# Weight sums moved to VectorE, residual rows scaled around an MLP in place of 1/rms inside it, and one more running sum through GpSimd

## The chip, the cores and the metric

The kernel runs on one core of a Trainium2 chip. The metric is the device time of one execution in microseconds (us), as the median of several runs. The engines are named as in the profile: PE is TensorE, DVE is VectorE, ACT is ScalarE, POOL is GpSimd, and SP issues most DMAs.

## The reference

One step of a two-layer streaming encoder over 1024 prompt frames and 32 sample frames, 1056 tokens of width 1024, all in float32. Each layer adds a token mixer and an MLP to the residual stream, both behind an RMS norm:

```python
def rmsnorm(x, g):
    y = x * lax.rsqrt(jnp.mean(x * x, axis=-1, keepdims=True) + EPS)
    return y * g
...
for i in range(DEPTH):                       # DEPTH = 2
    a = rmsnorm(h, norm_mix[i])
    h = h + mixer(a)                         # HGRN2 recurrence in layer 0, short convolution in layer 1
    m = rmsnorm(h, norm_mlp[i])
    h = h + jnp.square(jax.nn.relu(m @ w_up[i])) @ w_down[i]     # 1024 -> 4096 -> 1024
return rmsnorm(h, norm_final), ...
```

What matters here is the MLP. Its norm is a factor of one token: with v the mean square plus EPS, m is h times the norm's weights over sqrt(v). Relu and square carry a positive factor of a token through, so the square of the relu carries a factor 1/v.

## The kernel before

The tokens lie along the free axis, the features on the 128 partitions. The residual is eight tiles `hT[m]` of 128x1056. A float32 operand of a matmul is split in a high and a low part in `float32r` (`part`: ScalarE makes the high part as a cast, VectorE the low part as a difference), and a product is three matmuls (low times high, high times low, high times high; `mm3`, `mm_half`).

**The MLP.** The 4096 features are taken in 16 chunks of 256. A chunk has an `up` stage, which makes two tiles `u` of 128x1056, and two `down` stages, one for each half of the output features. Both use a Strassen scheme on 2x2 blocks, so they need sums of weight blocks (`wsums`) and sums of data blocks (`xsums`, called by `sums`). The order of the stages, written out at the end of `mlp`, is up(0), sums(0), up(1), down(0, 0), down(0, 1), sums(1), up(2), and so on. The loads and splits of a stage's weights are issued two stages ahead. Layer 0 ends with the last chunk in a plain product (`plain`), which hands each finished row of hT to the next norm and to the convolution; layer 1 ends with the last two chunks in a plain product over three groups of tokens (`groups`), behind which the final norm runs.

**`wsums`** loads 128x1024 weights (one of two `raw` tiles), splits the first half and the third quarter, then makes four sums of quarters (128x256) in place on GpSimd, and splits what they give. `whi` and `wlo` have seven buffers each.

**`up`** evicts eight results into four half tiles of `u` (`READ`): the first of a half is copied by ScalarE, later ones are added by VectorE, and when a half is complete VectorE takes relu and multiplies by 1/rms (`nrm.r`), and ScalarE squares. The chunk 0 of a layer is evicted raw and finished later, since its matmuls run before 1/rms is there: `nrm.scale`, called in the midst of chunk 0's matmuls, sums the squares over partitions by a matmul with ones and takes three Newton steps (`rsqrt`) on VectorE, each pass over 128x1056.

**`down`** computes seven products (`STEPS`) for two row halves p each, alternating p. PSUM has four tiles of two banks (`pb`). Products 0, 2, 4 and 6 of one p accumulate in tile a, 1 and 3 in tile b, and 5 is tile c. After each product its tile is read and added to, or subtracted from, a half row of hT (`TO` names row and half: product 0 and 5 go to block (0, 0), 2 and 3 to (0, 1), 1 and 4 to (1, 1), 6 to (1, 0)). VectorE does this straight from PSUM, except for products 0 and 6: ScalarE copies these to `st` (four buffers), and GpSimd adds them.

Each engine runs its own queue in order. The order in the queues is made by a planner from the order of the program, the dependencies and its own costs; only the start of the program (SP) is ordered by hand.

Of the kernel before, what the change touches and what calls it, by code (L numbers as in the profile page):

```python
# [8 lines left out]
F32 = mybir.dt.float32  # L9
# [4 lines left out]
AF = mybir.ActivationFunctionType  # L14
# [21 lines left out]
def trunk_kernel(  # L36
# [94 lines left out]
    def gsl(g):  # L131
        c0, n = GROUPS[g]
        return slice(c0, c0 + n), n
# [550 lines left out]
    class Norm:  # L684
# [13 lines left out]
                nc.gpsimd.tensor_tensor(self.acc, self.acc, sq, op=ALU.add)  # L698
            self.n += 1

        def scale(self):
            v = self.new("nv")
            _, pss = trio()
            for g in range(3):
                sl, n = gsl(g)
                ps = pss[g]
                nc.tensor.matmul(ps[:, :n], ones, self.acc[:, sl], start=True, stop=True)
                nc.vector.tensor_scalar(v[:, sl], ps[:, :n], 1.0 / D, EPS, op0=ALU.mult, op1=ALU.add)
            r = mp.tile([P, NTOK], F32, tag="nr", name="nr")
            rsqrt(v, r, self.acc)  # L710
            self.r = r
# [39 lines left out]
    def wsums(src):  # L751

        raw = wraw(src)
        t = lambda i: raw[:, i * 256 : (i + 1) * 256]
        hl = [wpart(raw[:, :512]), wpart(t(2))]
        for d, o in ((2, 3), (3, 0), (0, 2), (1, 0)):
            nc.gpsimd.tensor_tensor(t(d), t(d), t(o), op=ALU.add)  # L757
# [87 lines left out]
    def mlp(layer, nrm, on_final, last, X):  # L845
# [3 lines left out]
        def up(c):  # L849
            def run(w):  # L850
                u = [ut("u") for j in range(2)]
                left = {b: list(READ.values()).count(b) for b in READ.values()}
                made = set()

                def read(what, ps):
                    i, h = b = READ[what]
                    sl = slice(h * HALF, (h + 1) * HALF)
                    d = u[i][:, sl]
                    op0 = ALU.min if i else ALU.max
                    left[b] -= 1  # L860
                    src = d
                    if b in made:
                        nc.vector.tensor_tensor(q2(d), q2(d), ps, op=ALU.add)
                    elif left[b] or c == 0:
                        nc.scalar.copy(q2(d), ps)
                    else:
                        src = ps
                    made.add(b)
                    if not left[b]:
                        r = lambda: nrm.r[:, sl]  # L870

                        def end():
                            if src is d:
                                nc.vector.scalar_tensor_tensor(d, d, 0.0, r(), op0=op0, op1=ALU.mult)
                            else:
                                nc.vector.scalar_tensor_tensor(q2(d), src, 0.0, q2(r()), op0=op0, op1=ALU.mult)
                            if c:
                                nc.scalar.activation(d, d, AF.Square)
                            else:
                                nc.vector.tensor_tensor(d, d, d, op=ALU.mult)  # L880

                        later.append(end) if c == 0 else end()

                later = []
# [4 lines left out]
                for f in later:  # L889
                    f()  # L890
                U[c] = u

            return lambda: wpair(Wu[c]), run
# [9 lines left out]
        def down(c, b):  # L903
            def run(w):
                x = Z[c]
                ps = [{}, {}]
                for i, (bank, f, g, start) in enumerate(STEPS):
                    for p in range(2):
                        if start:
                            ps[p][bank] = pt()  # L910
                        t = ps[p][bank]
                        mm_half(t, w(f, p), x[g], start, True)
                        v = t[:, :, :QT]
                        r, h, op = TO[i]
                        d = hT[4 * b + 2 * p + r][:, h * HALF : (h + 1) * HALF]
                        if i in (0, 6):
                            st = mp.tile([P, HALF], F32, tag="st", name="st", bufs=4)
                            nc.scalar.copy(q2(st), v)  # L918
                            nc.gpsimd.tensor_tensor(d, d, st, op=op)  # L919
                        else:  # L920
                            nc.vector.tensor_tensor(q2(d), q2(d), v, op=op)  # L921

            return lambda: wsums(Wd[c, b]), run

        def wblocks(src):
# [2 lines left out]
            hl = [wpart(raw[:, i * 512 : (i + 1) * 512]) for i in range(2)]  # L928
            return lambda i, j, p: wcut(hl[BLK[(i, j)] // 2], BLK[(i, j)] % 2 * 2 + p)

        def plain(b):


            def run(w):
                for m in range(4 * b, 4 * b + 4):
                    a, pss = trio()
                    mm_groups(pss, [w(m % 2, j, m % 4 // 2) for j in range(2)], G)
                    nc.vector.tensor_tensor(two(hT[m]), two(hT[m]), a[:, :, :384], op=ALU.add)
                    nc.vector.tensor_tensor(hT[m][:, 768:], hT[m][:, 768:], pss[2][:, :288], op=ALU.add)
                    on_final(m)  # L940

            return lambda: wblocks(Wd[NFC - 1, b]), run
# [8 lines left out]
        def gsplit(u, new):  # L951
            h, l = [new(t, F32R) for t in ("gh", "gl")]
            part(h, l, u)
            G.append((h, l))


        def groups():


            n = NFC - 2  # L960

            def prep():
                wts = []
                for i in range(4):
                    raw = wraw(Wd[n + i % 2, i // 2])
                    h, l = [t[:, :1024] for t in xpair()]
                    part(h, l, raw)
                    wts.append((h, l))
                return wts

            def run(wts):
                for g in range(3):
                    c0, nt = FGROUPS[g]
                    sl = slice(c0, c0 + nt)
                    pss = {}
                    order = [(m, k) for m in range(KT) for k in range(4)]
                    if g == 0:
                        order = [(m, k) for m in range(4) for k in range(3)] + [(m, 3) for m in range(4)] + order[16:]
                    for m, k in order:
                        if k == 0:  # L980
                            pss[m] = newps()[:, :nt]
                        w = wcut(wts[m // 4 * 2 + k // 2], 2 * BLK[(m % 2, k % 2)] + m % 4 // 2)
                        gh, gl = G[k]
                        mm3(pss[m], *w, gh[:, sl], gl[:, sl], k == 0, k == 3)
                        if k == 3:
                            nc.vector.tensor_tensor(hT[m][:, sl], hT[m][:, sl], pss[m], op=ALU.add)
                            on_final(g, m)

            return prep, run
# [22 lines left out]
        ready = [work[0][0](), work[1][0]()]  # L1012
# [216 lines left out]
```

## Time and profile before

| what | value |
|---|---|
| median of 3 runs | 2498.72 us (2497.92 to 2499.29) |
| time of the profiled execution | 2497.78 us |
| its span | 2495.6 us |
| mean granted clock | 0.988 |
| busy PE, DVE, ACT, POOL | 2395.5, 1747.7, 917.1, 848.7 us |

The MLPs lie at about 625 to 1375 us and 1740 to 2495 us of the span. A row of a group of instructions gives line, engine, operation, written and read tiles with shapes and a count; behind the bar stand the busy time in us, the mean of one in ns, and the idle time of the engine just before these instructions with what ended it. A row of a timeline gives start and duration in us, and in brackets the idle time before it with its releaser. A row of waits gives who waited for whom, total us, times, and the longest.

### The profile page before, as it was taken

How to read it: one execution, taken by the hardware profiler on the slowest of the kernel's cores; microseconds unless marked ns; L12 is line 12 of the kernel's file. 1: busy time of each engine (PE TensorE's matmuls, PEld its weight loads, DVE VectorE, ACT ScalarE, POOL GpSimd, SP SyncE). 2: the span in 40 equal slices, each digit the busy share in tenths (PEclk: the TensorE clock that was granted, in tenths of full speed). 3: DMA queues.
4: the chain of work that ended last, by engine and by line, in shares of the span. 5: the costliest groups of instructions: out<-in, count | busy, mean ns of one | idle time of the engine just before them, and what ended most of it. 6: DMA issues, size and time to landing. Idle time of an engine off the chain costs nothing.

```text
span 2495.6 us, 42858 instructions
## 1 busy us (share of the span) xinstructions
PE 2395.5 (96%) x17700; PEld 2345.9 (94%) x17700; DVE 1747.7 (70%) x2842; ACT 917.1 (37%) x1671; POOL 848.7 (34%) x920
## 2 busy tenths in 40 slices
PE   8999999989899999999999999999999999999998
PEld 8999999989899999999999999999999999999997
DVE  8775757554878777787788633354887787787875
ACT  5121212133344444444445111143344444444444
POOL 3110101012255454545555000002255554555433
PEclk9999999999999999999999999999999999999999
DMA  4111010031011111111111111111111111111111
GB/s 148 38 32 44 29 46 23 28 114 38 32 47 47 52 52 43 43 52 43 50 45 51 51 51 44 43 51 35 35 51 43 43 52 44 54 49 43 51 52 70
DMA packets 35779, 122.22 MB, mean 49 GB/s; under 512 B 4336, under 2 KB 7552, under 8 KB 35584
## 3 DMA queue, kind: packets, MB, share of 16 engines
q1 hardware_dynamic: 33632, 113.58, 14.5%
q0 software_dynamic: 1952, 5.92, 0.6%
q8 instruction: 138, 2.26, 0.4%
q14 instruction: 57, 0.47, 0.1%
HBM read 114.09 MB, written 5.39 MB: 48 GB/s over the span
## 4 chain that ended last, share of the span: by engine, by line
PE 74%; POOL 8%; issue 8%; DVE 8%; ACT 2%; DMA 0%; DVEq 0%; SPq 0%; POOLq 0%; ACTq 0%
PE pb L807 34%; PE pb L115 6%; PE pb L117 6%; PE pb L116 6%; POOL hT L919 6%; PE pj L115 4%; PE pj L116 3%; PE pj L117 3%; DVE wlo L601 2%; POOL raw L757 2%; PE v L501 1%; PE v L503 1%; PE v L502 1%; PE aps L394 1%; ACT whi L600 1%
## 5 line engine op out<-in xcount | busy, mean ns | idle before, releaser
L600 ACT CAST whi<-raw 128x512 fp32r<-128x512 f32 (+1 forms) x476 | 275.3, 580 | 867.0 <-PE pb L807 450.5
L757 POOL TENSOR_TENSOR raw<-raw 128x256 f32<-128x256 f32 x360 | 371.4, 1032 | 365.5 <-DVE wlo L601 237.7
L601 DVE TENSOR_TENSOR wlo<-raw,whi 128x512 fp32r<-128x512 f32 (+1 forms) x476 | 362.4, 763 | 186.7 <-ACT whi L600 180.9
L919 POOL TENSOR_TENSOR hT<-hT,st 128x528 f32<-128x528 f32 x232 | 329.4, 1431 | 335.9 <-ACT st L918 335.9
L921 DVE TENSOR_TENSOR hT<-hT,pb 128x528 f32<-128x528 f32 x580 | 387.4, 696 | 19.5 <-PE pb L807 14.5
L807 PE MATMUL pb<-B,whi 128*128 128x264 f32 x2160 | 356.0, 287 | 0.0
L115 PE MATMUL pb<-xh,wlo 128*128 128x384 f32 (+1 forms) x960 | 312.3, 325 | 5.8 <-DVE wlo L601 5.8
L117 PE MATMUL pb<-xh,whi 128*128 128x384 f32 (+1 forms) x960 | 310.9, 324 | 0.0
L116 PE MATMUL pb<-xl,whi 128*128 128x384 f32 (+1 forms) x960 | 309.9, 323 | 0.8 <-DVE xl L604 0.8
L807 PEld LDWEIGHTS pb<-B,whi 128*128 128x128 f32 x2160 | 303.5, 191 | 0.0
L807 PE MATMUL pb<-B,wlo 128*128 128x264 f32 x1080 | 228.0, 293 | 11.5 <-DVE hT L921 7.6
L807 PE MATMUL pb<-T,whi 128*128 128x264 f32 x1440 | 238.2, 288 | 0.0
L807 PE MATMUL pb<-Q,whi 128*128 128x264 f32 x1440 | 235.1, 285 | 0.0
L807 PE MATMUL pb<-xh,wlo 128*128 128x264 f32 x1024 | 208.4, 285 | 0.0
L807 PE MATMUL pb<-xl,whi 128*128 128x264 f32 x1024 | 208.2, 285 | 0.0
L807 PE MATMUL pb<-xh,whi 128*128 128x264 f32 x1024 | 207.7, 284 | 0.0
L807 PEld LDWEIGHTS pb<-T,whi 128*128 128x128 f32 x1440 | 203.9, 193 | 0.0
L807 PEld LDWEIGHTS pb<-Q,whi 128*128 128x128 f32 x1440 | 200.5, 190 | 0.0
L807 PE MATMUL pb<-Q,wlo 128*128 128x264 f32 x720 | 150.9, 291 | 42.3 <-ACT st L918 42.3
L807 PEld LDWEIGHTS pb<-B,wlo 128*128 128x128 f32 x1080 | 169.0, 190 | 23.6 <-DVE hT L921 18.3
L115 PEld LDWEIGHTS pb<-xh,wlo 128*128 128x128 f32 x960 | 181.0, 189 | 6.2 <-issue 5.9
L115 PE MATMUL pj<-xh,wlo 128*128 128x384 f32 (+1 forms) x536 | 176.6, 330 | 6.7 <-ACT xh L192 6.7
(265 smaller groups left out, 4857.3 us busy)
## 6 DMA issues: line engine op xcount, KB each, us to landing
raw<-in_wg_up_dram SPq DMA_DIRECT2D x64, 512.0 KB, 3.5
raw<-in_wg_down_dram SPq DMA_DIRECT2D x64, 512.0 KB, 3.6
raw<-in_wg_in_hgrn_dram SPq DMA_DIRECT2D x31, 512.0 KB, 4.1
raw<-in_wg_cu_conv_dram SPq DMA_DIRECT2D x16, 512.0 KB, 3.5
xk<-in_x_t_dram SPq DMA_DIRECT2D x8, 528.0 KB, 8.2
hT<-in_x_t_dram POOLq DMA_DIRECT2D x8, 528.0 KB, 8.1
raw<-in_wg_out_hgrn_dram SPq DMA_DIRECT2D x8, 512.0 KB, 4.6
raw<-in_wg_b_conv_dram SPq DMA_DIRECT2D x8, 512.0 KB, 3.4
```

Of the source, the lines that this page charges most:

```text
L115: nc.tensor.matmul(ps, wlo, ah, start=start, stop=False)
L116: nc.tensor.matmul(ps, whi, al, start=False, stop=False)
L117: nc.tensor.matmul(ps, whi, ah, start=False, stop=stop)
L394: nc.tensor.matmul(o, H.K[:, sl], H.F[:, sl], start=True, stop=True)
L501: nc.tensor.matmul(o, al, hi[:, kk], start=(k == 0), stop=False)
L502: nc.tensor.matmul(o, ah, lo[:, kk], start=False, stop=False)
L600: nc.scalar.copy(h, src)
L601: nc.vector.tensor_tensor(l, src, h.bitcast(F32), op=ALU.subtract)
L757: nc.gpsimd.tensor_tensor(t(d), t(d), t(o), op=ALU.add)
L807: nc.tensor.matmul(ps[:, q, :QT], w, half(v, q), start=start and n == 0, stop=stop and n == 2, skip_group_check=True)
L919: nc.gpsimd.tensor_tensor(d, d, st, op=op)
L921: nc.vector.tensor_tensor(q2(d), q2(d), v, op=op)
```

## The change

With v the mean square of a token, the kernel now keeps v itself (`nrm.mean`) and no 1/rms in an MLP. The up stages take relu of the raw result (the negated half through a scale of -1) and square it, both on ScalarE, in chunk 0 as in the others. The result of the down products is then too large by v for each token, so all eight rows of hT are multiplied by v on GpSimd, behind chunk 0's up stage and ahead of the first running sum, and at the end multiplied by 1/v: `inverse` makes the reciprocal in place on VectorE, and `plain` and `groups` multiply behind each last eviction. `Norm.scale` stays for the convolution's norm. Besides, the four sums of `wsums` are on VectorE instead of GpSimd, and product 2 of a `down` stage goes through ScalarE and GpSimd like 0 and 6.

```diff
+        def mean(self):
+            v = mp.tile([P, NTOK], F32, tag="nr", name="nr")
+            self.means(v)
+            self.v = v
+
+        def means(self, v):
             _, pss = trio()
             for g in range(3):
                 ...
                 nc.tensor.matmul(ps[:, :n], ones, self.acc[:, sl], start=True, stop=True)
                 nc.vector.tensor_scalar(v[:, sl], ps[:, :n], 1.0 / D, EPS, op0=ALU.mult, op1=ALU.add)
 ...
         for d, o in ((2, 3), (3, 0), (0, 2), (1, 0)):
-            nc.gpsimd.tensor_tensor(t(d), t(d), t(o), op=ALU.add)
+            nc.vector.tensor_tensor(t(d), t(d), t(o), op=ALU.add)
 ...
-                    elif left[b] or c == 0:
+                    elif left[b]:
 ...
                     if not left[b]:
-                        ...  nc.vector.scalar_tensor_tensor(d, d, 0.0, r(), op0=op0, op1=ALU.mult)
-                        ...  nc.scalar.activation(d, d, AF.Square)      # chunk 0: on VectorE, later
+                        nc.scalar.activation(q2(d), src, AF.Relu, scale=-1.0 if i else 1.0)
+                        nc.scalar.activation(d, d, AF.Square)
 ...
-                    mm_pair(w, X, read, LATE, {2: nrm.scale})
+                    mm_pair(w, X, read, LATE, {2: nrm.mean})
+                    for m in range(KT):
+                        nc.gpsimd.tensor_tensor(hT[m], hT[m], nrm.v, op=ALU.mult)
 ...
-                        if i in (0, 6):
+                        if i in (0, 2, 6):
                             st = mp.tile([P, HALF], F32, tag="st", name="st", bufs=4)
                             nc.scalar.copy(q2(st), v)
                             nc.gpsimd.tensor_tensor(d, d, st, op=op)
 ...
+        def inverse():
+            for g in range(3):
+                sl, _ = gsl(g)
+                nc.vector.reciprocal(nrm.v[:, sl], nrm.v[:, sl])
 ...                                                     # plain
+                    nc.vector.tensor_tensor(hT[m], hT[m], nrm.v, op=ALU.mult)
                     on_final(m)
 ...                                                     # groups
+                            nc.vector.tensor_tensor(hT[m][:, sl], hT[m][:, sl], nrm.v[:, sl], op=ALU.mult)
                             on_final(g, m)
 ...                                                     # stages: last layer, first layer
+            stages.append(inverse)
             stages.append(up(n + 1))
 ...
-            stages += [down(n - 1, 1), plain(0), plain(1)]
+            stages += [down(n - 1, 1), inverse, plain(0), plain(1)]
```

More of the change, by code (lines that the diff above doesn't have):

```diff
@@ L699, in add @@
             self.n += 1
-        def scale(self):
-            v = self.new("nv")
+        def mean(self):
[3 more added lines that the diff above has]
+        def means(self, v):
             _, pss = trio()
@@ L708, in scale @@
                 nc.vector.tensor_scalar(v[:, sl], ps[:, :n], 1.0 / D, EPS, op0=ALU.mult, op1=ALU.add)
+        def scale(self):
+            v = self.new("nv")
+            self.means(v)
             r = mp.tile([P, NTOK], F32, tag="nr", name="nr")
@@ L856, in read @@
                     i, h = b = READ[what]
-                    sl = slice(h * HALF, (h + 1) * HALF)
-                    d = u[i][:, sl]
-                    op0 = ALU.min if i else ALU.max
+                    d = u[i][:, h * HALF : (h + 1) * HALF]
                     left[b] -= 1
-                    src = d
+                    src = q2(d)
                     if b in made:
-                        nc.vector.tensor_tensor(q2(d), q2(d), ps, op=ALU.add)
-                    elif left[b] or c == 0:
-                        nc.scalar.copy(q2(d), ps)
+                        nc.vector.tensor_tensor(src, src, ps, op=ALU.add)
+                    elif left[b]:
+                        nc.scalar.copy(src, ps)
                     else:
```

14 lines of the change are left out of this document (removed).

## The prediction

> **What bounds the kernel now.** The page's first part comes first: it says which engine the time belongs to.
>
> ```profile
> span 2495.6 us, 42858 instructions
> PE 2395.5 (96%) x17700; PEld 2345.9 (94%) x17700; DVE 1747.7 (70%) x2842; ACT 917.1 (37%) x1671; POOL 848.7 (34%) x920
> ```
>
> TensorE (PE) is busy for 2395.5 of 2495.6 us, so about 100 us of idle time is all that any schedule can win, unless it takes matmuls away, which this change does not. Where the 100 us lie, the windows over single chunks and the list of waits say (in a window row the columns are length, then PE, weight load, VectorE, ScalarE and GpSimd busy time, granted clock, DMA share and rate; in a wait row total, times, longest).
>
> ```profile
> 818.96:863.92 44.96, 43.17 (x351) 42.53 (x350) 35.42 (x54) 20.49 (x37) 23.57 (x20) 1.00 0.15 48
> 1843.00:1888.00 45.00, 43.20 (x351) 42.56 (x351) 35.55 (x54) 20.58 (x38) 23.61 (x21) 1.00 0.15 48
> ...
> PE pb L807 <- ACT st L918: 42.3, 28, 1.5
> PEld pb L807 <- DVE hT L921: 18.9, 51, 0.6
> ACT whi L600 <- POOL raw L757: 83.1, 34, 2.6
> ```
>
> A chunk of an MLP takes 45.0 us, of which PE idles 1.8. There are 29 chunks with a down stage (232 GpSimd running sums, 8 per chunk, in the group rows below), so 52 us of the 100 are this one stall. The timeline of one chunk shows what it is made of:
>
> ```profile
> 869.08 0.69 DVE L601 TENSOR_TENSOR wlo<-raw,whi 128x512 fp32r<-128x512 f32 x1
> ...
> 875.94 0.74 POOL L757 TENSOR_TENSOR raw<-raw 128x256 f32<-128x256 f32 x1
> 876.62 1.31 POOL L919 TENSOR_TENSOR hT<-hT,st 128x528 f32<-128x528 f32 x1
> 876.71 0.62 ACT L600 CAST whi<-raw 128x512 fp32r<-128x512 f32 x1 [2.58 <-POOL raw L757]
> 877.24 0.59 ACT L918 COPY st<-pb 128x528 f32<-128x528 f32 x1
> 877.36 1.12 DVE L601 TENSOR_TENSOR wlo<-raw,whi 128x512 fp32r<-128x512 f32 x1 [4.20 <-ACT whi L600]
> 877.88 0.51 PE L807 MATMUL pb<-Q,wlo 128*128 128x264 f32 x2 [1.51 <-ACT st L918]
> ```
>
> The cast of summed weights stands ahead of an eviction copy in ScalarE's queue and waits 2.58 us for GpSimd's weight sums; the copy behind it is late, so PE waits 1.51 us for its PSUM bank, and VectorE, 4.20 us idle, then evicts late (the short waits on L921).
>
> **The change part by part.** The durations (busy us, mean ns):
>
> ```profile
> L921 DVE TENSOR_TENSOR hT<-hT,pb 128x528 f32<-128x528 f32 x580 | 387.4, 696 | 19.5 <-PE pb L807 14.5
> L757 POOL TENSOR_TENSOR raw<-raw 128x256 f32<-128x256 f32 x360 | 371.4, 1032 | 365.5 <-DVE wlo L601 237.7 <-issue 111.0
> L919 POOL TENSOR_TENSOR hT<-hT,st 128x528 f32<-128x528 f32 x232 | 329.4, 1431 | 335.9 <-ACT st L918 335.9
> L918 ACT COPY st<-pb 128x528 f32<-128x528 f32 x232 | 136.0, 598 | 20.6 <-PE pb L807 15.1
> L601 DVE TENSOR_TENSOR wlo<-raw,whi 128x256 fp32r<-128x256 f32 x90 | 37.4, 416 | 5.2 <-ACT whi L600 5.2
> L874 DVE SCALAR_TENSOR_TENSOR u<-u,nr 128x528 f32<-128x528 f32 x98 | 69.3, 711 | 0.2
> L878 ACT ACTIVATE u<-u 128x528 f32<-128x528 f32 x120 | 77.6, 647 | 48.4 <-DVE u L874 46.4 <-DVE u L876 1.9
> L698 POOL TENSOR_TENSOR acc<-acc,sq 128x1056 f32<-128x1056 f32 x21 | 54.5, 2597 | 178.2 <-ACT sq L697 178.1
> L285 DVE RECIPROCAL R<-F 128x384 f32<-128x384 f32 x16 | 40.1, 2530 | 0.2
> ```
>
> Budget of a steady chunk. VectorE: 12 weight sums come (three weight sets of four; priced like the 128x256 split, 0.416) = +5.0; four evictions go to ScalarE = -2.8; four relu-times-1/rms go = -2.8: together -0.6 of 35.4. GpSimd: 12 x 1.032 go, 4 x 1.431 come = -6.7 of 23.6. ScalarE: 4 x 0.598 + 4 relu at the price of a square, 0.647 = +5.0 on 20.5, of 45. No engine becomes the bound by its total, so the sum is decided by waits.
>
> *The wait that goes.* The sums follow the 128x256 split on VectorE without another engine in between, some 0.34 us apart, so the cast is ready about 2 us earlier and the 1.8 us per chunk disappear. What is late next is the point.
>
> *The wait that comes.* In a down stage PE computes seven products for each of two row halves, alternating. Product 2 and product 3 both add into the same block (0, 1) of hT. Before, VectorE did both. Now product 2 goes ScalarE copy, GpSimd add, and VectorE's add of product 3 must wait for that add. Product 5 needs the PSUM tile that this add of product 3 releases (four tiles: two hold products 0, 2, 4, 6 to the end, two are product 1 and 3's). So each half has a new chain GpSimd to VectorE to PE, and the next evictions are queued behind the blocked one on VectorE. Its clock comes from these rows:
>
> ```profile
> 885.27 22.92 PE pb L807 x186
> ...
> 863.65 0.31 PEld L807 LDWEIGHTS pb<-Q,wlo 128*128 128x128 f32 x2
> 863.92 2.81 POOL L919 TENSOR_TENSOR hT<-hT,st 128x528 f32<-128x528 f32 x2 [0.20 <-ACT st L918]
> 864.69 4.36 DVE L921 TENSOR_TENSOR hT<-hT,pb 128x528 f32<-128x528 f32 x6 [0.43 <-PE pb L807]
> 874.65 1.34 POOL L919 TENSOR_TENSOR hT<-hT,st 128x528 f32<-128x528 f32 x1
> 885.56 3.20 POOL L919 TENSOR_TENSOR hT<-hT,st 128x528 f32<-128x528 f32 x2 [4.38 <-ACT st L918]
> ```
>
> PE needs 6 x 22.92/186 = 0.74 us for a product of one half, and a product is ready 1.04 us after its load begins (863.65 to 864.69). GpSimd adds follow each other every 1.29 us when undisturbed (874.65 to 875.94).
>
> Second down of a chunk, with 0 where its first product is ready: the preceding down's two last products are ready at -1.48 and -0.74 and go to GpSimd too. Six adds, the first at -0.86 (copy 0.6), end at -0.86 + 6 x 1.29 = 6.9; VectorE's add of product 3, second half, ends at 7.6; PE wants the tile for product 5, second half, at 11 x 0.74 - 1.04 = 7.1. Stall 0.5 at least.
>
> Now the port. At 877.36 the split took 1.12 us where the 128x512 form took 0.69 at 869.08: it ended 0.55 us after GpSimd's add that ran until 877.93. The reverse is seen here:
>
> ```profile
> 892.33 0.41 DVE L601 TENSOR_TENSOR wlo<-raw,whi 128x256 fp32r<-128x256 f32 x1
> 892.67 0.69 DVE L776 TENSOR_TENSOR u<-u 128x528 f32<-128x528 f32 x1
> 892.88 2.95 POOL L757 TENSOR_TENSOR raw<-raw 128x256 f32<-128x256 f32 x1 [4.11 <-issue]
> ```
>
> A 0.74 us add took 2.95 us while VectorE streamed SBUF sums. The four new weight sums (start to start 0.34, as 892.33 to 892.67) and a split (about 0.6) fall into that second down and hold GpSimd off by up to 4 x 0.34 + 0.6 = 2.0 us: stall 0.5 to 2.5. I take 2.0, since the 128x256 split that they follow ends just before that stage's first product. The Trainium skill, "SBUF — State Buffer", section "Who interferes with whom", says that a VectorE instruction with two SBUF inputs and a GpSimd instruction that reads SBUF exclude each other, the later one blocking fully; 1.12 against 0.69 agrees. By that rule the stall is at the 2.5 end, without it at 0.5, and the total moves between +35 and -23 us for the 29 chunks.
>
> First down of a chunk: only four adds, from about 1.2 after its own zero (its copies now stand behind a relu in ScalarE): end 6.4, VectorE 7.1, wanted 7.1: stall 0 to 0.5, taken 0.2. Its last evictions follow later and the next down's first tile needs them: 0 to 1.0, taken 0.3.
>
> Sum per chunk: 2.5 (0.5 to 4.0) comes, 1.8 goes: +0.7 (-1.3 to +2.2), times 29 = **+20 us** (-38 to +64).
>
> *MLP heads.* The mean replaces the rsqrt: nine VectorE passes of 128x1056 (1.25 us each, the row of L147 below) go, 11 us, and the first chunk's four squarings. There PE waits:
>
> ```profile
> PE pb L707 <- POOL acc L698: 5.2, 1, 5.2
> PE pb L807 <- DVE u L863: 2.4, 2, 1.9
> ```
>
> The 5.2 us stay: the sum of squares still ends on GpSimd, and the matmul for the mean keeps its place. The 2.4 go. Against them come eight GpSimd products of hT and the mean, priced as L698, 21 us, before the first down, on the port that the splits and sums use: taken as 0 net, -5 to +10 for both heads.
>
> *End of layer 0.* The last down is the plain product, eight rows of hT:
>
> ```profile
> 1325.00:1371.00 46.00, 44.07 (x292) 43.05 (x291) 41.49 (x46) 26.32 (x33) 25.93 (x13) 1.00 0.17 56
> L604 DVE SCALAR_TENSOR_TENSOR xl<-hT,vec,xh 128x1056 fp32r<-128x1056 f32 x8 | 18.4, 2303 | 1.0 <-ACT xh L603 1.0
> L147 DVE TENSOR_TENSOR acc<-nv,nr 128x1056 f32<-128x1056 f32 x9 | 11.3, 1253 | 0.2
> ```
>
> VectorE is busy 41.5 of 46 here, and its split of a row takes 2.3 us, being held by GpSimd's sums of squares. Eight products of a row, priced at the 1.25 of the same shape, stand between eviction and split, and the convolution cannot start its last row before: +10 us, 5 where PE's own queue hides half, 17 if the three reciprocals (2.53 each, 7 with the narrow one) fall here. I expect those earlier, in VectorE's gaps: +1 for both layers.
>
> *End of layer 1.* 24 products, one behind each eviction:
>
> ```profile
> 2440.00:2460.00 20.00, 20.00 (x121) 19.59 (x120) 11.09 (x32) 10.78 (x20) 2.23 (x3) 1.00 0.02 6
> 2481.93 0.41 DVE L986 TENSOR_TENSOR hT<-hT,pb 128x256 f32<-128x256 f32 x1
> ```
>
> VectorE has 9 of 20 us free, so PE hides most; the last one, 0.41 like the eviction, is in the tail. +2 (0.4 to 5).
>
> Sum: 20 + 0 + 10 + 1 + 2 = +33 us on the profiled execution's 2497.8 (2.2 of it outside the span) = 2531; the median of the runs shown is 0.9 higher, so 2532.
>
> **The rivals.** *Faster: the queue stall goes and GpSimd delivers in time.* If the weight sums land after the six adds, the chunk's stall is 0.5 + 0.2 + 0.1 = 0.8, -1.0 x 29 = -29; heads -5, end of layer 0 +5: 2470. For it speaks that GpSimd's total falls by 6.7 us a chunk; against it that six adds in a row leave no reserve even undisturbed (7.6 against 7.1). It decides from a stall below 1.4 us per chunk, where 29 x 0.4 pay for the 12 us at the ends.
>
> *VectorE's queue becomes the bound in the down stages.* If a split or sum is queued between the two adds of product 3, the late evictions pile up: the stall reaches 4.0, +64, with 15 at the end of layer 0: 2579. For it speaks that its evictions run at PE's own pace now (six in 4.36 us, 0.73 each); against it the 2 us gap that the moved product 2 leaves.
>
> *Nothing to measure.* 1.4 us per chunk cancels the ends: 2499. It needs a coincidence.
>
> **How the numbers follow.** A measurement can tell about 0.2%, 5 us. Chances: forecast and neighbourhood (2512 to 2555) 0.40, VectorE's queue 0.17, no change 0.10, faster 0.33. Likeliest 2532, alone 2512 to 2555. For 8 in 10 the range must take in most of both rivals: 2468 to 2570.
>
> **What would show it.** In the changed profile the wait of the cast on L757's GpSimd sums is gone; a wait of VectorE's L921 on GpSimd's L919 appears, some 58 to 116 times, and PE waits on L921 grow from 18.9 us to 50 or more; a chunk takes 45.7 us (45.0 now); the stretch from the last down of layer 0 to the convolution grows by 10 us. I am wrong if chunks fall below 44.5 us: then either the adds are not held, or the order on VectorE puts the sums elsewhere. If the end of layer 0 does not grow, VectorE had more room there than 41.5 of 46 says.

## The result, and the profile after

| | before | after |
|---|---|---|
| median | 2498.6 us (4 runs) | 2653.16 us (4 runs, 2649.05 to 2655.59) |
| ratio, 95% interval | | 1.0617 (1.0599 to 1.0635) |
| profiled execution: time, span | 2497.78, 2495.6 us | 2653.62, 2651.8 us |
| mean granted clock | 0.988 | 0.959 |

The change costs 154 us. The forecast was 2532 us, at most 2570: the direction was right, the size was not. The first part of the page after:

```profile
span 2651.8 us, 43088 instructions
PE 2467.1 (93%) x17700; PEld 2407.9 (91%) x17700; DVE 1871.5 (71%) x2968; ACT 1059.9 (40%) x1921; POOL 705.1 (27%) x692
```

TensorE has the same 17700 matmuls, yet it is busy for 72 us longer (2467.1 against 2395.5): part of its work ran slower. The rest of the 156 us is idle time. GpSimd is less busy than before (705 against 849 us), VectorE more by 124 us. That last number is the surprise, since the forecast's budget had VectorE 0.6 us a chunk lower. The groups say where it comes from (busy us, mean ns, then idle):

```profile
L915 POOL TENSOR_TENSOR hT<-hT,st 128x528 f32<-128x528 f32 x348 | 504.6, 1475 | 921.6 <-ACT st L914 918.5
L917 DVE TENSOR_TENSOR hT<-hT,pb 128x528 f32<-128x528 f32 x464 | 318.3, 699 | 163.9 <-PE pb L816 82.7
L766 DVE TENSOR_TENSOR raw<-raw 128x256 f32<-128x256 f32 x360 | 250.0, 695 | 7.1
```

A weight sum takes 0.695 us on average, where 0.416 was assumed; the evictions (L917) kept their 0.70.

The matmuls come in the same order in all kernels here, so two traces can be laid side by side at the n-th matmul. The table gives the time of a stretch of matmuls, less that of the kernel before, in us. The experiments are in it too. A chunk is 348 matmuls, so each column of chunks holds about 13 of them. Left out are the stretch between head and chunks of layer 0 (matmul 4560 to 5040), from -4.7 to +0.9, the one between the layers (10080 to 12240), from -0.8 to +4.4, and what lies ahead of the first head, at most 2.0 either way.

| kernel | head, layer 0 (4320-4560) | 13 chunks (5040-9600) | end, layer 0 (9600-10080) | head, layer 1 (12240-12720) | 13 chunks (12720-17280) | last part (17280-17699) |
|---|---|---|---|---|---|---|
| before, us | 30.1 | 595.5 | 80.6 | 66.2 | 592.5 | 67.6 |
| **after** | **+11.5** | **+53.6** | **+11.6** | **+11.2** | **+55.9** | **+10.7** |
| e1_sums_on_pool | +12.8 | +40.5 | +11.6 | +11.8 | +40.1 | +11.8 |
| e2_products06 | +11.6 | +18.8 | +8.4 | +8.2 | +22.0 | +10.2 |
| e3_sums_only | -0.6 | +19.7 | 0.0 | -0.2 | +19.7 | 0.0 |
| e4_norm_only | +12.8 | +3.4 | +8.9 | +9.5 | +3.6 | +11.8 |
| e5_no_sums | +10.8 | +0.7 | +11.8 | +7.2 | +1.2 | +8.1 |
| e6_late_inverse | +8.8 | +3.4 | +16.9 | +4.1 | +3.2 | +11.8 |
| e7_half_sums | +10.6 | +19.2 | +12.2 | +7.3 | +20.0 | +10.5 |
| e8_free_start | +11.6 | -5.5 | +10.8 | +8.4 | -4.4 | +10.7 |
| e9_pool_order | -0.7 | -35.0 | 0.0 | -2.4 | -34.2 | 0.0 |
| e10_head_halves | +10.9 | +53.9 | +11.7 | +6.6 | +54.4 | +12.4 |
| e11_no_products | -0.7 | +53.5 | +11.7 | -0.2 | +54.8 | +9.5 |
| e12_no_division | +3.3 | +54.8 | +3.5 | +2.8 | +54.5 | +0.1 |

So 110 of the 156 us lie in the steady chunks, and the heads and ends cost 45 us.

**A chunk.** Windows of ten chunks of layer 0, from the 5448th matmul on (length, then PE, weight load, VectorE, ScalarE, GpSimd busy; granted clock; DMA share and rate), before and after:

```profile
788.90:1242.39 453.49, 435.64 (x3481) 429.87 (x3481) 356.96 (x531) 204.64 (x360) 235.21 (x201) 0.99 0.16 47
```

```profile
808.67:1303.50 494.83, 455.49 (x3481) 447.00 (x3481) 394.23 (x570) 250.02 (x440) 173.43 (x120) 0.95 0.14 43
```

A chunk grew from 45.35 to 49.48 us: TensorE idles 3.93 us instead of 1.79 in it, and is busy 1.99 us longer, at a lower clock. The waits (total, times, longest) of after name who makes it idle:

```profile
PEld pb L816 <- DVE hT L917: 116.7, 91, 3.3
PE pb L816 <- DVE hT L917: 94.3, 61, 3.1
DVE hT L917 <- POOL hT L915: 80.4, 60, 2.6
PE pb L816 <- ACT st L914: 14.7, 28, 0.5
...
ACT whi L600 <- DVE raw L766: 49.4, 32, 1.6
```

TensorE waits for VectorE's evictions: 28 pauses of about 3.1 us, one in a second down stage of a chunk, make up 86.5 of the 94.3 us. The timeline of VectorE and GpSimd around one such pause:

```profile
798.87 0.70 DVE L917 TENSOR_TENSOR hT<-hT,pb 128x528 f32<-128x528 f32 x1
799.49 5.33 DVE L766 TENSOR_TENSOR raw<-raw 128x256 f32<-128x256 f32 x4
804.73 1.78 DVE L601 TENSOR_TENSOR wlo<-raw,whi 128x512 fp32r<-128x512 f32 x1
806.44 1.30 DVE L917 TENSOR_TENSOR hT<-hT,pb 128x528 f32<-128x528 f32 x2
...
798.59 9.09 POOL L915 TENSOR_TENSOR hT<-hT,st 128x528 f32<-128x528 f32 x6 [3.76 <-ACT st L914]
...
803.13 1.40 POOL L915 TENSOR_TENSOR hT<-hT,st 128x528 f32<-128x528 f32 x1
803.40 1.42 DVE L766 TENSOR_TENSOR raw<-raw 128x256 f32<-128x256 f32 x1
...
836.30 1.81 DVE L766 TENSOR_TENSOR raw<-raw 128x256 f32<-128x256 f32 x4
...
807.18 0.81 PE L816 MATMUL pb<-B,wlo 128*128 128x264 f32 x2 [3.09 <-DVE hT L917]
```

The four weight sums of the next up stage take 5.33 us here and 1.81 us where GpSimd is idle (836.30). Look at the single pair: GpSimd's add runs from 803.13 to 804.53, VectorE's sum is issued at 803.40 and ends at 804.82, just behind it. Each sum, and the split behind them, waits out one GpSimd add (the first sum, which takes 0.95 us, only the rest of one). The evictions of product 1 stand behind these five instructions in VectorE's queue and start at 806.44, and TensorE has been idle for 3.09 us by then. An eviction, which reads PSUM, runs at its full speed while GpSimd's last add goes on (806.44, two in 1.30 us).

The same pause in windows of 2 us shows what follows it:

```profile
802.00:804.00 2.00, 1.50 (x11) 1.17 (x10) 1.97 (x2) 1.56 (x3) 1.95 (x2) 1.00 0.00 0
804.00:806.00 2.00, 0.09 (x1) 0.00 (x0) 2.00 (x2) 0.60 (x1) 2.00 (x3) 1.00 0.00 0
806.00:808.00 2.00, 0.82 (x3) 0.82 (x4) 1.74 (x3) 0.00 (x0) 1.68 (x1) 0.55 0.00 0
808.00:810.00 2.00, 2.00 (x11) 2.00 (x11) 0.70 (x1) 0.00 (x0) 0.00 (x0) 0.50 0.00 0
810.00:812.00 2.00, 2.00 (x11) 2.00 (x11) 1.70 (x3) 0.62 (x1) 0.00 (x0) 0.50 0.00 0
812.00:814.00 2.00, 2.00 (x14) 2.00 (x14) 1.38 (x3) 1.13 (x2) 0.00 (x0) 0.75 0.41 156
814.00:816.00 2.00, 2.00 (x19) 2.00 (x18) 1.70 (x4) 1.56 (x4) 0.00 (x0) 1.00 0.26 107
```

From the end of the pause on the granted clock is 0.50 for nearly 7 us, and TensorE starts 11 matmuls in 2 us instead of 19. In the ten chunks of the windows the clock stood at one half for 51.1 us, and for 10.0 us before. Half of the 41 us more is 20.5 us, close to the 19.9 us that TensorE was busy longer.

### The profile page after: what moved, and what is told of

The parts are those of the page before. It is cut to its first block, busy times and chain, and to the rows that moved or that the text cites. A ratio compares the mean times of both kernels' runs of the same rounds, so it can differ in the third digit from the quotient of the medians.

```text
span 2651.8 us, 43088 instructions
## 1 busy us (share of the span) xinstructions
PE 2467.1 (93%) x17700; PEld 2407.9 (91%) x17700; DVE 1871.5 (71%) x2968; ACT 1059.9 (40%) x1921; POOL 705.1 (27%) x692
## 4 chain that ended last, share of the span: by engine, by line
PE 64%; DVE 15%; issue 11%; POOL 7%; ACT 1%; DMA 0%; DVEq 0%; SPq 0%; ACTq 0%; POOLq 0%
PE pb L816 27%; PE pb L115 6%; PE pb L117 6%; PE pb L116 6%; POOL hT L915 5%; DVE raw L766 4%; DVE wlo L601 4%; DVE hT L917 3%; PE pj L115 3%; PE pj L116 3%; PE pj L117 3%; POOL hT L886 2%; PE v L501 1%; PE v L503 1%; PE v L502 1%
## 5 line engine op out<-in xcount | busy, mean ns | idle before, releaser
L915 POOL TENSOR_TENSOR hT<-hT,st 128x528 f32<-128x528 f32 x348 | 504.6, 1475 | 921.6 <-ACT st L914 918.5
L601 DVE TENSOR_TENSOR wlo<-raw,whi 128x512 fp32r<-128x512 f32 (+1 forms) x476 | 383.8, 808 | 136.9 <-ACT whi L600 136.2
L917 DVE TENSOR_TENSOR hT<-hT,pb 128x528 f32<-128x528 f32 x464 | 318.3, 699 | 163.9 <-PE pb L816 82.7
L816 PE MATMUL pb<-B,whi 128*128 128x264 f32 x2160 | 375.8, 299 | 0.0
L816 PE MATMUL pb<-B,wlo 128*128 128x264 f32 x1080 | 244.5, 310 | 90.9 <-DVE hT L917 87.7
L816 PEld LDWEIGHTS pb<-B,whi 128*128 128x128 f32 x2160 | 325.5, 204 | 0.0
L766 DVE TENSOR_TENSOR raw<-raw 128x256 f32<-128x256 f32 x360 | 250.0, 695 | 7.1
L914 ACT COPY st<-pb 128x528 f32<-128x528 f32 x348 | 202.9, 599 | 95.8 <-PE pb L816 87.6
L816 PE MATMUL pb<-xh,wlo 128*128 128x264 f32 x1024 | 209.5, 286 | 12.8 <-DVE u L870 12.8
L816 PEld LDWEIGHTS pb<-T,whi 128*128 128x128 f32 x1440 | 217.2, 205 | 0.0
L116 PEld LDWEIGHTS pb<-xl,whi 128*128 128x128 f32 x960 | 182.0, 190 | 4.4 <-DVE xl L604 4.1
```

The lines of the kernel that those rows point to most:

```text
L116: nc.tensor.matmul(ps, whi, al, start=False, stop=False)
L601: nc.vector.tensor_tensor(l, src, h.bitcast(F32), op=ALU.subtract)
L766: nc.vector.tensor_tensor(t(d), t(d), t(o), op=ALU.add)
L816: nc.tensor.matmul(ps[:, q, :QT], w, half(v, q), start=start and n == 0, stop=stop and n == 2, skip_group_check=True)
```

## The experiments

The theory behind all of them (A): VectorE's weight sums alternate with GpSimd's running adds in the second down stage. The rivals: the moved product 2 alone makes the stall; VectorE simply has too much in its queue; the new norm upsets the chunks.

**e1_sums_on_pool**: the sums back on GpSimd.

```diff
-            nc.vector.tensor_tensor(t(d), t(d), t(o), op=ALU.add)
+            nc.gpsimd.tensor_tensor(t(d), t(d), t(o), op=ALU.add)
```

> The changed kernel with only the weight sums back on GpSimd. Theory A (port): in the second down stage of a chunk the four weight sums of the next up stage each wait on VectorE for one GpSimd running add (1.43 us instead of 0.41), product 1's evictions stand behind them, PE waits 3.1 us and its granted clock halves for 3.4 to 6.8 us afterwards. Without sums on VectorE that wait goes, but GpSimd then has six adds and four sums in one row, at least 6 x 1.29 + 4 x 0.70 = 10.5 us, so the add of product 3 comes about 3 us late by the chain of product 2: chunk 46.5 to 49 us, total 2590 to 2650. Theory B (the recorded one: the chain of product 2 alone makes the loss): the same or worse than the changed kernel, chunk 49 to 51, total 2650 to 2700. If the sums' move alone were the cause: chunk 45, total about 2545 (2499 and the 45 us that the heads and the ends lost).

Measured: 2627.88 us, ratio 1.0522 (1.0492 to 1.0553). The chunks still lose 81 of 110 us. With sums and twelve adds a chunk on one queue, GpSimd itself is late: VectorE waits 179.9 us on it, 116 times, where it was 80.4 us. TensorE waits 45.1 us for the evictions behind that, and 40.3 us for ScalarE's copies, nearly as before the change (42.3): with the sums back on GpSimd the old stall is back too. So product 2 is no harmless part; who makes the sums only decides how it is paid.

**e2_products06**: product 2 back on VectorE, the sums stay there.

```diff
-                        if i in (0, 2, 6):
+                        if i in (0, 6):
```

> The changed kernel with product 2 evicted by VectorE again (GpSimd adds only products 0 and 6). Theory A: the four sums still meet four GpSimd adds (products 6 of the first down, products 0 of the second), so they still take some 5 us and PE still waits: chunk 47.5 to 49, total 2600 to 2650. Theory B: the chain that it names is gone, chunk at most 45, total at most 2545.

Measured: 2575.02 us, 1.0311 (1.0281 to 1.0341). The chunks lose 41 us, 1.6 each: the sums alone, against GpSimd's adds of products 0 and 6, make TensorE wait up to 2.0 us in one piece. The time lies between the two expectations: the chain of product 2 is gone and a loss stays, as A had it, but a smaller one (a chunk of 46.9 us, where A had 47.5 to 49).

**e3_sums_only**: the kernel before with the sums on VectorE and nothing else.

> The kernel before with only the weight sums moved to VectorE. Theory A: the sums meet GpSimd's adds as in the changed kernel: chunk 47.5 to 49, granted clock below 0.97, total 2570 to 2615. Theory B: the wait of the cast on GpSimd's sums (1.8 us a chunk) goes and nothing comes: chunk at most 45, total 2450 to 2500.

Measured: 2535.96 us, 1.0154 (1.0125 to 1.0184), all of it in the chunks (+39 us), nothing at heads and ends. This too lies between the expectations, with a chunk of 46.8 us. The chunks of e2 and e3 agree within 2.3 us per layer, so the new norm has no part in them.

**e5_no_sums**: the changed kernel without the four sums (their work is left out).

> The changed kernel with the four weight sums left out (the products then use unsummed weights; only the time is read). Theory A: VectorE's queue is free for the evictions, what is left is the chain of product 2, at most 1 us of PE waits: chunk 43.5 to 44.5, granted clock 0.98 or more, total 2500 to 2530. Theory B: the chain of product 2 keeps its 2 us or more: chunk 45 or more, total at least 2545.

Measured: 2534.66 us, 1.0149 (1.0120 to 1.0178). The chunks cost what they cost before. Its window of ten chunks and the wait of TensorE:

```profile
794.60:1248.39 453.79, 441.36 (x3482) 427.95 (x3481) 302.30 (x450) 251.72 (x441) 172.35 (x121) 1.00 0.15 47
```

```profile
PE pb L814 <- DVE hT L915: 30.3, 117, 0.6
```

Product 2's chain by itself makes many short waits of at most 0.6 us, in place of the old stall, and 45.38 us a chunk against 45.35. That is longer than A had it (43.5 to 44.5; the time too is 5 us above its range), so A priced this chain too low. The step to 49.48 needs both: product 2 on GpSimd, and the sums.

**e4_norm_only**: both edits undone, only the new norm is left.

> The changed kernel with the weight sums back on GpSimd and product 2 back on VectorE: only the new norm (rows scaled by the mean square, divided behind the MLP) is left of the change. Theory A (GpSimd's adds hold back VectorE's weight sums one for one in the second down stage, and product 1's evictions stand behind them): without sums on VectorE and with two products on GpSimd the chunks of both layers cost what they cost before, about 45.0 us each, so the loss against the kernel before at equal matmul number does not grow between matmul 4560 and 9600 (at most 5 us, where the changed kernel grew by 54), and what is left is the two MLP heads (7 to 12 us each), the end of layer 0 (8 to 12) and the end of layer 1 (7 to 9): some 2530 to 2540 us. Rival (the recorded one, VectorE's queue full of evictions because the relu moved from VectorE to ScalarE changes their order): the chunks still lose 1 us or more each, and the time is above 2555.

Measured: 2542.2 us, 1.0177 (1.0156 to 1.0197). Chunks +3.4 and +3.6 us for thirteen, heads and ends +43 us. The rival that the norm upsets the chunks falls. The sum came out 2 us above the expected interval.

**e7_half_sums**: each sum of the changed kernel in two halves.

```diff
+            for q in range(2):
+                c = slice(q * 128, q * 128 + 128)
+                nc.vector.tensor_tensor(t(d)[:, c], t(d)[:, c], t(o)[:, c], op=ALU.add)
```

> The changed kernel with each weight sum on VectorE written as two instructions of 128x128 in place of one of 128x256: the same elements, eight instructions instead of four. Theory A (in the second down stage VectorE gets one instruction in for each GpSimd add, whatever its size): the sums take longer there, six to eight waits of about 1.4 us instead of four as long as GpSimd has adds to alternate with, TensorE's idle piece of 3.09 us becomes 4 to 7 us, and the time is 25 to 90 us above the changed kernel's 2653. Rival (GpSimd's adds slow VectorE by a rate, so that the cost goes with the elements): only the fixed cost of four more instructions, at most 0.5 us a chunk, 2650 to 2668 us.

Measured: 2573.75 us, 1.0303 (1.0282 to 1.0323): 79 us *faster* than the changed kernel, where either theory had the same or slower. VectorE, GpSimd and ScalarE at the same place:

```profile
793.45 2.74 DVE L768 TENSOR_TENSOR raw<-raw 128x128 f32<-128x128 f32 x2
...
796.11 1.09 DVE L768 TENSOR_TENSOR raw<-raw 128x128 f32<-128x128 f32 x5
...
791.81 4.23 POOL L917 TENSOR_TENSOR hT<-hT,st 128x528 f32<-128x528 f32 x3 [3.76 <-ACT st L916]
797.62 2.65 POOL L917 TENSOR_TENSOR hT<-hT,st 128x528 f32<-128x528 f32 x2 [1.58 <-ACT st L916]
...
796.42 0.62 ACT L600 CAST whi<-raw 128x512 fp32r<-128x512 f32 x1 [2.85 <-DVE raw L768]
796.95 1.10 ACT L916 COPY st<-pb 128x528 f32<-128x528 f32 x2
```

The alternation is there and goes by instruction, not by size: the second and the third half take 2.74 us together, each as long as a whole sum. But GpSimd has only three adds ready. The copy for the fourth stands in ScalarE's queue behind a cast that waits for the second sum (2.85 us), and until 797.62 GpSimd has nothing to do: the other five halves take 1.09 us together. In the changed kernel the second sum, one instruction, was done 3.3 us after the first add began instead of 4.6, so the cast and the copies behind it were earlier, GpSimd's fourth add followed at 803.13 without a break, and the last sum and the split had to wait as well. So A's rule held and the forecast from it failed, since it took for granted that GpSimd always has an add ready. What is left of the loss is another wait: TensorE waits 49.9 us for ScalarE's copies, up to 1.8 us in one piece, since they stand behind that cast.

**e8_free_start**: product 0 of the second down stage stays on VectorE, so that GpSimd has only two adds, of the stage before, to meet the sums.

```diff
-                        if i in (0, 2, 6):
+                        if i in ((2, 6) if b else (0, 2, 6)):
```

> The changed kernel, but in the second down stage of a chunk product 0 stays on VectorE; GpSimd keeps products 2 and 6 there and products 0, 2, 6 in the first down stage. So GpSimd has no add ready while VectorE makes the four weight sums of the next up stage, and VectorE has two evictions of 0.70 us more to do at that place. Theory A (each sum waits for one GpSimd add of 1.4 us to end): the sums take 0.4 us each again, TensorE's idle piece of 3.1 us becomes at most 1 us, the granted clock is not halved behind it, and a chunk costs 45 to 46 us instead of 48.7: 2540 to 2580 us. Rival (VectorE simply has too much queued ahead of product 1's evictions, whatever GpSimd does): two more evictions ahead make it no shorter: 2645 to 2700 us.

Measured: 2532.75 us, 1.0136 (1.0057 to 1.0214; its two runs are 16 us apart, and the rows are of the faster), a little below the expected 2540 to 2580. The chunks are now *shorter* than before, by 5.5 and 4.4 us per layer, against +54 and +56:

```profile
795.97:1245.87 449.90, 438.07 (x3482) 428.32 (x3481) 364.82 (x590) 241.32 (x420) 142.04 (x101) 1.00 0.15 48
```

```profile
790.41 0.95 DVE L766 TENSOR_TENSOR raw<-raw 128x256 f32<-128x256 f32 x1
...
791.90 0.93 DVE L766 TENSOR_TENSOR raw<-raw 128x256 f32<-128x256 f32 x1
...
793.37 0.41 DVE L766 TENSOR_TENSOR raw<-raw 128x256 f32<-128x256 f32 x1
...
794.30 0.41 DVE L766 TENSOR_TENSOR raw<-raw 128x256 f32<-128x256 f32 x1
```

VectorE has two evictions more to do, yet the loss is gone: the amount of work in VectorE's queue was not the cause. The first two sums still meet GpSimd's adds of the stage before (0.95 and 0.93 us), the others run at 0.41. The planner also put evictions between the sums here, so part of the gain may be that order; the two weren't taken apart.

**e6_late_inverse**: as e4, with the reciprocals behind VectorE's last eviction of the preceding down stage.

```diff
+            with tc.issue_after(mark["dve"].ins):
+                for g in range(3):
...
+                    nc.vector.reciprocal(nrm.v[:, sl], nrm.v[:, sl])
```

> The kernel with the new norm alone (sums on GpSimd, products 0 and 6 there), with the three reciprocals put behind VectorE's last eviction of the preceding down stage instead of behind GpSimd's eight products of the head. If the heads lose because the reciprocals stand in VectorE's queue waiting for GpSimd's products (7.2 us at L930 in the changed kernel) and TensorE waits on the evictions behind them (6.4 us in one piece), then 5 us or more of each head's 7 to 12 come back; the reciprocals (5.0 + 1.9 us) now lie ahead of the plain stages of layer 0, where VectorE is full, and can cost up to 7 us there: net 3 to 15 us faster than the norm alone. If the heads lose to something else (the products' hold on the port, the missing overlap of the norm), the heads stay where they are and the time is that of the norm alone, or up to 7 us above.

Measured: 2545.08 us, 1.0188 (1.0168 to 1.0208), 3 us above e4 instead of below. The heads gave back 4.0 and 5.4 us, but the end of layer 0 lost 8.0 more, where the reciprocals now lie. The heads still lose 8.8 and 4.1 us: in the first, TensorE's longest wait fell from 10.5 us in e4 to 6.9, though no reciprocal stands there any more. What makes that rest wasn't taken apart.

**e10_head_halves**: the eight products of the head in sixteen halves.

> The changed kernel with GpSimd's eight products of an MLP's head written as sixteen of 128x528 in place of eight of 128x1056: the same elements. In the changed kernel they take 21.3 us, and VectorE gets in one instruction on buffer memory for each of them. If a VectorE instruction waits for one GpSimd instruction to end, the waits halve (1.3 us instead of 2.6 us) and VectorE gets through twice as much: each head loses 2 to 6 us less against the kernel before (11.2 and 11.2 us between matmuls 4320 and 4560, and 12240 and 12720), 2641 to 2650 us. Rival (VectorE gets a share of the time): the heads stay within 1.5 us of the changed kernel's, 2650 to 2656 us. The planner may set the reciprocals elsewhere; where TensorE waits says if it does.

Measured: 2653.03 us, 1.0617 (1.0587 to 1.0648), no change. The time tells nothing on the alternation: the planner set the first reciprocal amid the products (a wait of 6.27 us of VectorE on GpSimd before the second), so the queue is another one. The trace does tell: splits of 128x512 that took 2.73 and 2.95 us beside whole products in the changed kernel take 1.80 and 1.81 us beside half ones. The wait goes by the length of GpSimd's instruction.

**e11_no_products** and **e12_no_division**: the changed kernel without the head's products, and without reciprocals and divisions.

> The changed kernel without GpSimd's eight products of the head: the rows are not multiplied by the mean square ahead of the MLP (the division behind it stays), so part of the computation is left out. If the products' hold on VectorE is the heads' cost, each head loses at most 3 us against the kernel before (11.2 us in the changed kernel), 2628 to 2640 us; if the reciprocals' own 7 us on VectorE are, 6 us or more of each head's loss stay, above 2640 us. The chunks and the ends stay as in the changed kernel.

> The changed kernel without the division behind the MLP: neither the reciprocals nor the multiplications of the rows in the end of layer 0 and in the end of layer 1 are done, so part of the computation is left out; the products of the head stay. If VectorE's multiplications and the reciprocals are what the ends lose, the end of layer 0 loses at most 2 us against the kernel before (12 us in the changed kernel, between matmuls 9600 and 10080) and the last part of layer 1 at most 2 us (9 us from matmul 17280 on), and the heads lose 3 to 7 us less than the changed kernel's 11: 2615 to 2635 us. If the ends stay, something else in them is the cause: 2640 us or more.

Measured: 2626.79 us, 1.0512 (1.0482 to 1.0543), and 2617.33 us, 1.0474 (1.0444 to 1.0505). Without the products both heads cost what they cost before (-0.7 and -0.2 us), though the reciprocals run. Without the reciprocals they cost +3.3 and +2.8, so they got back 8 us each, more than the 3 to 7 expected. So most of the price in the changed kernel is the meeting of the two, seen in its head:

```profile
642.41 21.30 POOL L886 TENSOR_TENSOR hT<-hT,nr 128x1056 f32<-128x1056 f32 x8 [10.28 <-DVE nr L713]
...
642.70 5.60 DVE L601 TENSOR_TENSOR wlo<-raw,whi 128x512 fp32r<-128x512 f32 x2 [0.37 <-ACT whi L600]
...
663.74 4.96 DVE L930 RECIPROCAL nr<-nr 128x384 f32<-128x384 f32 x2 [7.21 <-POOL hT L886]
...
669.17 0.69 DVE L870 TENSOR_TENSOR u<-u,pb 128x528 f32<-128x528 f32 x1
...
669.92 0.81 PE L816 MATMUL pb<-xh,wlo 128*128 128x264 f32 x2 [6.40 <-DVE u L870]
```

The reciprocal overwrites the mean that the products read, so it can't start before the last product ends. The planner put it in VectorE's queue ahead of an eviction, VectorE stood for 7.21 us and took 5 more for two reciprocals, and TensorE waited 6.40 us for that eviction. The end of layer 0 falls from +11.6 to +3.5 without division (at most 2 was expected; what the 3.5 are stays open), the last part from +10.7 to +0.1.

**e9_pool_order**: the kernel *before*, with GpSimd's first add of product 6 in the first down stage put behind the second weight sum in GpSimd's queue.

```diff
+                            if (b, i, p) == (0, 6, 0):
+                                with tc.issue_after(second["up"].ins):
+                                    add()
```

> The kernel before, with one edit: GpSimd's first add of product 6 in the first down stage is put behind the second of the next weight's sums in GpSimd's queue, so that the sums (and the splits behind them) are not held back by the add that waits for ScalarE's copy. If the old stall of 1.8 us a chunk (TensorE on the wait for the second operand's split) is due to this order on GpSimd, it goes: 29 chunks at 1.0 to 1.8 us, 2446 to 2470 us. Rival: the add that is put back comes late for VectorE's last product, and the wait moves to the second down stage's start at about the same price: 2490 to 2505 us.

Measured: 2424.91 us, 0.9706 (0.9690 to 0.9722): 73 us faster than before and 228 us faster than the changed kernel. Ten chunks:

```profile
783.79:1210.67 426.88, 426.88 (x3482) 424.84 (x3481) 355.80 (x531) 203.93 (x360) 240.01 (x201) 1.00 0.16 50
```

TensorE is busy for 426.88 of 426.88 us. GpSimd's order before was add, sum, add, sum (827.71 to 831.66), and is now two sums first:

```profile
827.71 1.33 POOL L919 TENSOR_TENSOR hT<-hT,st 128x528 f32<-128x528 f32 x1 [5.95 <-ACT st L918]
829.00 0.74 POOL L757 TENSOR_TENSOR raw<-raw 128x256 f32<-128x256 f32 x1
829.70 1.32 POOL L919 TENSOR_TENSOR hT<-hT,st 128x528 f32<-128x528 f32 x1
830.98 0.73 POOL L757 TENSOR_TENSOR raw<-raw 128x256 f32<-128x256 f32 x1
```

```profile
821.39 1.55 POOL L759 TENSOR_TENSOR raw<-raw 128x256 f32<-128x256 f32 x2 [5.91 <-DVE wlo L601]
822.90 1.32 POOL L924 TENSOR_TENSOR hT<-hT,st 128x528 f32<-128x528 f32 x1
```

The gain went 21 us beyond the expectation, which counted the idle time alone: of the 2.66 us a chunk in these rows 1.79 are idle time, and 0.88 come from TensorE's being less long busy. The half clock of before, 10.0 us in ten chunks, accounts for 0.5 of these; what the rest is wasn't taken apart.

## Why the prediction was wrong, step by step

- **The wait that goes**: right in the main. TensorE's wait on ScalarE's copies fell from 42.3 to 14.7 us. The rest stays because the cast now waits for the sums on VectorE (49.4 us, where it waited 83.1 for GpSimd).
- **The wait that comes, product 2's chain**: the mechanism was right, as e5 shows, where no sums disturb it. In the second down stage of a chunk TensorE has waits of 0.28, 0.27 and 0.22 us (0.5 was forecast without the port), in the first one of 0.22 us (0.2). By e5 the chain without sums just makes up for the old stall, 1.8 us, where the forecast's terms without the port came to 1.0. But the two signs named for it came true in the changed kernel in part by luck. Of VectorE's 60 waits on GpSimd (58 to 116 were named), 56 lie in the first down stages, not in the second, where the forecast had its stall; and TensorE's 94.3 us of waits on evictions (50 or more were named) are nearly all the pauses behind the sums.
- **The port, the step that failed.** The forecast let the sums hold GpSimd's adds off, by 1.5 us a chunk, and let TensorE wait for those adds. The adds did become slower, about as forecast: six take 9.09 us in the rows above, where 6 x 1.29 is 7.74. But TensorE doesn't wait for them there. GpSimd's adds hold the sums longer still (5.33 instead of 1.81 us, and 1.78 for the split behind them), and product 1's evictions stand behind the sums. From e5 to the changed kernel this term costs 4.1 us a chunk, 2.7 of idle time and 1.4 of longer busy time. The row that was read for the size, a GpSimd add of 2.95 us beside VectorE's stream, shows the other case: three VectorE instructions that started after it, at 892.88, went ahead of it.

```profile
893.29 0.69 DVE L601 TENSOR_TENSOR Q<-u,Q 128x528 fp32r<-128x528 f32 x1
893.91 0.69 DVE L776 TENSOR_TENSOR u<-u 128x528 f32<-128x528 f32 x1
894.52 0.69 DVE L601 TENSOR_TENSOR Q<-u,Q 128x528 fp32r<-128x528 f32 x1
```

There VectorE's stream was running when GpSimd's add came; in the changed kernel six GpSimd adds follow one another, and five instructions of VectorE got one turn each. What decides between the two cases, no run here shows. The row named ahead of it, a split of 1.12 instead of 0.69 us behind a GpSimd add, was the nearer one. The Trainium skill, "SBUF — State Buffer", section "Who interferes with whom", which the prediction used, also says that issue order decides who blocks. For the sums the trace agrees (1.42 instead of 0.41 us for a sum, behind an add of 1.40 that started before it); for the add at 892.88 it doesn't, since the three that went ahead started later.

- **The clock, a term left out.** The forecast priced idle time at its own length. Each long pause cost as much again: 2.1 us a chunk more idle time came with 2.0 us of matmuls at a lower clock. The prediction's first paragraph is too narrow as well, where it lets a schedule win idle time alone: in e9, with the same 17700 matmuls, TensorE's busy time fell from 2395.5 to 2375.3 us.
- **Steady chunks in all**: +0.7 us a chunk forecast, +4.1 measured (+20 us for 29 chunks, and +110 for the 26 of the table). The rival of VectorE's queue came nearest: its stall of up to 4.0 us is about what TensorE idles, 3.9. It had the sums between the two adds of product 3, though, and they stood ahead of product 1's evictions; and its 2579 us lacked the clock and the heads.
- **Heads**: 0 forecast, +11.5 and +11.2 measured. What was missed is less the products' price (3.3 and 2.8 us without the reciprocals) than that the reciprocals depend on them and stand in VectorE's queue ("earlier, in VectorE's gaps", +1).
- **End of layer 0**: +10 forecast, +11.6 measured, mostly by the mechanism named: without the division 3.5 are left.
- **End of layer 1**: +2 (0.4 to 5) forecast, +10.7 measured. The multiplications there delay the final norm's sum, on which TensorE now waits, and the clock falls to 0.88 in that stretch, from 0.92. The waits:

```profile
PE pb L163 <- DVE facc L1104: 7.3, 3, 3.4
```

The same row of before has 0.6 us. That VectorE was free for 9 of 20 us didn't help an instruction on the chain.

## What to carry to other kernels

When work moves between two engines that hold each other up at the buffer memory, ask in which order their ready instructions will meet, and count turns as well as microseconds: behind GpSimd adds that followed one another, a short instruction of VectorE cost one whole add each. Price a pause of TensorE with the clock that follows it. Where a stall comes from the order of one queue, try that order first: one reordered add on GpSimd gained 73 us, where moving the sums to another engine lost 39 by itself (e3), and 154 with the rest of the change. And where a step overwrites what another engine still reads, look at what is queued behind it.

## What the runs showed of the hardware

The turns were not expected: while GpSimd's adds followed one another, VectorE instructions with both inputs in buffer memory went one for one with them, sums of 128x256 and of 128x128 alike (1.4 us each). It is no rule for both sides: in the kernel before, 27 GpSimd sums that met VectorE's running stream let three VectorE instructions pass, as at 892.88.

The clock was sharper than expected. All TensorE pauses from 640 us on in the fourteen traces, and how many had the granted clock fall to 0.50 in them or within 1.5 us of their end:

| pause, us | 0.3 to 1.0 | 1.0 to 1.5 | 1.5 to 2.0 | 2.0 to 3.0 | from 3.0 |
|---|---|---|---|---|---|
| pauses | 317 | 57 | 184 | 40 | 169 |
| half clock follows | 16 | 4 | 54 | 19 | 168 |

The half clock lasted 3.41 us or two or three times that, except for the last one of each trace (12.0 to 14.9 us, at the end of the program). The table fits that the old pause of 1.5 us did little harm and that one of 3.1 us costs double. The Trainium skill, "TensorE: Matmul & The Clock Gate", section "Part 1: The HAM clock gate", names a free-running window of 3413 ns and half rate after an idle window; the length agrees (3.41 us in the records), but pauses below a whole window sufficed: of the 169 from 3.0 us on, 129 were shorter than 3.41 us, and half clock followed all but one; of those from 1.5 to 2.0 us it followed 54 of 184.
